# Seven products of halves in the projection of the layer embedding

## The chip, the core and the metric

The kernel runs on one core of a Trainium2 chip. The metric is the device time of one execution in microseconds (us), taken as the median of several runs of the same program. A separate execution was recorded by the hardware profiler, and every duration of a single instruction in this document comes from such a recorded execution. Engines are named as in the profile: PE (TensorE matmul), PEld (its weight load), DVE (VectorE), ACT (ScalarE), POOL (GpSimd), SP (the engine that issues all DMAs here).

## The reference, cut to what matters

The kernel computes one decoder layer on 1024 tokens of width 1024: a norm, an input projection, a mixture of dilated attention and a spatial gating unit, an output projection, a feed-forward network, and at the end a gated addition of a per-token layer embedding. The change touches the last factor of the last line:

```
h = h + rmsnorm(mixed, ln_post_mix[i])
...
h = h + rmsnorm(y, ln_post_ffn[i])
gate = jax.nn.sigmoid(h @ w_pe_gate[i] + b_pe_gate[i])
h = h + gate * (p[i] @ w_pe_proj[i])
```

`p[i]` is 1024 x 256 and `w_pe_proj[i]` is 256 x 1024, in 32-bit floats. This product depends on nothing else in the layer, so it can be computed at any time before the end.

## The kernel before, in words

Tokens are cut into eight row tiles of 128. A product of two float32 matrices is made of three matmuls on split operands: each operand is split into a rounded high part (an ACT copy into a rounding type) and the remainder as low part (a DVE subtraction), and `mm3` (L521) issues high x high, high x low and low x high into the same PSUM bank. A matmul takes a stationary operand of 128x128 and a moving one of up to 128x512.

Most products of the kernel also use a scheme with seven products of halves in place of eight: both matrices are cut into 2x2 blocks, some sums and differences of blocks are formed, seven block products are computed in the order `ORDER = (1, 2, 6, 5, 7, 3, 4)` (L660), and their results are added up in two PSUM banks and in SBUF. `winograd_b` (L650) forms the sums of the second operand in place, with four block additions. `gated(pair)` (L1063) does this for the spatial-gating half of the output projection, for two row tiles at a time.

The projection of the layer embedding did not use the scheme. `ple(t)` (L1125) handles one row tile t. It loads the 128x256 rows of p, transposes the two 128x128 blocks on PE, splits the result, and for each of the two column halves of 512 issues two `mm3` calls (one for each block of the contraction) into a bank of the group "fill". ACT copies the bank to SBUF, and SP stores it into the DRAM tensor `ppd`, which `embed` (L1462) reads at the end of the kernel. The first call also loads and splits w_pe_proj: four 512-wide splits.

The order of instructions is not written out by hand. The functions record operations in a graph, and a planner (`Graph.order`, L225) replays it on the host with priced operations and fixes one order for each engine. Its `pick` (L283) takes, on a free engine, the first operation in recorded order that is ready and whose tiles fit; for PE it looks at up to 80 waiting operations, for DVE and ACT at 40, and nothing further than 400 operations past the oldest unfinished one may take new tiles (L122 to L124). SBUF tiles come from pools: 47 tiles of kind M (4 KB in each partition) and 14 of kind S (2 KB); PSUM has 8 banks, kind P. Some groups have a limit of tiles at once, "fill" three banks (L1513).

What stands around the change is the attention. It is done for four pairs of heads: first the first 512 tokens (`first_half`, L1289, for pr 0 to 3), then the other 512 (`second_half`, L1304, with the steps "far", 2 and 3). After each unit of attention some independent work is recorded behind it, as filler: `fed` (L1285) advances generators, `feed` (L1267) counts down the numbers that they yield. The generator `others` (L1326) holds `gated` and `ple`. A first half feeds `FA` times 0.15 twice and `FA` times 0.35 twice; a second half feeds `FO` times 0.15, 0.12 and 0.23, twice each. `gated` yields 6 for each of its seven products (six matmuls each), `ple` yielded 7 for each column half (six matmuls and a transpose). A second filler, `ahead` (L1339, the first products of the gate and up projections), becomes available only after the far step of the second pair of heads, when the first four row tiles have gone through `attn_out` (L1148), `h_chain` (L1159) and `F.first2` (L591). What is left of `ahead` runs afterwards.

Of the kernel before, what the change touches and what calls it, by code (L numbers as in the profile page):

```python
# [12 lines left out]
F32R = mybir.dt.float32r  # L13
# [4 lines left out]
P = 128  # L18
S = 1024
D = 1024  # L20
NT = S // P
# [7 lines left out]
PLE = 256  # L29
# [3 lines left out]
LO, HI = slice(0, 512), slice(512, 1024)  # L33
ADD, SUB, MUL = ALU.add, ALU.subtract, ALU.mult
# [357 lines left out]
def hybrid_block(ctx: ExitStack, tc, a, out):  # L392
    G = Graph()

    def M(dt=F32, shape=(P, 1024), group=None):
        return G.buf("M", shape, dt, group)

    def SM(dt=F32, shape=(P, 512), group=None):
        return G.buf("S", shape, dt, group)

    def PB(shape=(P, 512), group=None):
        return G.buf("P", shape, F32, group)
# [4 lines left out]
    def C(shape):  # L407
        return G.buf("C", shape)
# [4 lines left out]
    def pe(what, *args, **kw):  # L413
        return G.call("tensor", what, *args, **kw)
# [4 lines left out]
    def load(dst, src, rate=1.0):  # L419
        o = G.call("sync", "dma_start", dst, src)  # L420
        o.bytes /= rate
        return o

    def tt(dst, x, y, op=ADD, engines="vector"):
        return G.call(engines, "tensor_tensor", out=dst, in0=x, in1=y, op=op)

    def copy(dst, src):
        return G.call("scalar", "copy", dst, src)
# [4 lines left out]
    def split(hi, lo, x, engines="vector"):  # L433
        copy(hi, x)
        tt(lo, x, hi.f32(), SUB, engines)
# [6 lines left out]
    w_pg, w_pp = a["w_pe_gate"][0], a["w_pe_proj"][0]  # L442

    def rows(w, k0, nk, c0, ncol):
        return w[k0 * P : (k0 + nk) * P, c0 : c0 + ncol].rearrange("(k p) n -> p k n", p=P)
# [9 lines left out]
    def piece_r(w, k0):  # L455

        return (1024, [rows(w, k0 + i, 1, 0, 1024) for i in range(2)])
# [31 lines left out]
    def weights(piece, gains=None):  # L489
        return split_raw(load_raw(piece), piece[0], "vector", gains)  # L490


    ident, mhalf = C([P, P]), C([P, 8])
# [27 lines left out]
    def mm3(ps, l, r, first, last, **kw):  # L521
        pe("matmul", ps, l[0], r[0], start=first, stop=False, **kw)
        pe("matmul", ps, l[0], r[1], start=False, stop=False, **kw)
        pe("matmul", ps, l[1], r[0], start=False, stop=last, **kw)

    def gemm(ps, terms):
        for i, (l, r) in enumerate(terms):
            mm3(ps, l, r, i == 0, i == len(terms) - 1)
        return ps
# [120 lines left out]
    def winograd_b(q, b, tmp):  # L650

        if q == 6:
            tt(b(0, 1), b(1, 1), b(0, 1), SUB)
            tt(b(0, 0), b(0, 1), b(0, 0))
        if q == 5:
            tt(tmp, b(1, 1), b(0, 0), SUB)
            tt(b(1, 0), b(1, 0), b(0, 0), SUB)
        return tmp if q == 5 else b(*{1: (0, 0), 2: (1, 0), 3: (1, 1), 4: (1, 0), 6: (0, 0), 7: (0, 1)}[q])

    ORDER = (1, 2, 6, 5, 7, 3, 4)  # L660


    x = a["x"][0]
# [63 lines left out]
    ppd, h1d = DR([S, D]), DR([S, D])  # L727
# [100 lines left out]
    for q, banks in in_products(2048, 1536, zu_mm):  # L828
        for i in range(4):
            if q in (1, 6, 5):  # L830
                v, t = {1: (zs, i), 6: (us, i), 5: (us, i + 4)}[q]
# [5 lines left out]
            else:  # L837
                v = {2: zs, 3: us}.get(q, us)[i + 4 * (q == 7)]
# [6 lines left out]
            if q in (3, 4):  # L845
                t = i + 4 * (q == 4)
# [273 lines left out]
                tt(dst, bank, dst)  # L1120
            yield 6

    p, wpp = a["p"][0][0], []

    def ple(t):  # L1125
        if t == 0:
            wpp.extend(weights(piece_r(w_pp, 0)))
        pt = SM()[:, :PLE]
        load(pt, p[t * P : (t + 1) * P, :])
        ps = PB((P, 2, P), "fill")  # L1130
        for k in range(2):
            pe("transpose", ps[:, k, :], pt[:, k * P : (k + 1) * P], ident)
        pair = SM(F32R, (P, 2, PLE))
        split(pair[:, 0], pair[:, 1], ps.flat())
        for cs in (LO, HI):
            ps = gemm(PB(group="fill"), [
                (tuple(pair[:, i, k * P : (k + 1) * P] for i in range(2)), tuple(v[:, cs] for v in wpp[k]))
                for k in range(2)
            ])
            pp = SM()  # L1140
            copy(pp, ps)
            load(ppd[t * P : (t + 1) * P, cs], pp)
            yield 7


    F, kept = Feat(), {}
# [37 lines left out]
                skip_group_check=True)  # L1184

    EARLY = 20
    FB, FH, FF2, FA, FO = 36, 0, 48, 30, 105
    TODO = (((0, "far"), ("h", 0)), ((0, "far"), ("h", 1)), ((0, 2), ("h", 2)), ((0, 2), ("h", 3)), ((1, "far"), ("f", 0)),
            ((1, "far"), ("f", 1)))
    ed = {n: DR([2 * P, 512]) for n in range(EARLY)}  # L1190
# [72 lines left out]
    def chain(*gens):  # L1263
        for g in gens:
            yield from g
# [38 lines left out]
    def second_half(pr, fills, then):  # L1304
# [10 lines left out]
        for step in ("far", 2, 3):  # L1315
# [6 lines left out]
            if step in then:  # L1322
                then[step]()
        merge(pr)

    others = chain(*(gated(i) for i in range(2)), *(ple(t) for t in range(2)), *(gated(i) for i in range(2, 4)),  # L1326
                   *(ple(t) for t in range(2, NT)))

    def rows_out(*ts):
        for t in ts:  # L1330
# [63 lines left out]
    one = [PB() for _ in range(4)]  # L1394
    for q in ORDER:
        if q in (2, 5):
            two = [PB() for _ in range(4)]
        banks = two if q in (2, 5, 3) else one
        for g in range(NG):
            for j, c in USED.get(q, ()):  # L1400
                cs = slice(c * 512, (c + 1) * 512)
# [4 lines left out]
            s = winograd_b(q, lambda j, c: w_raw[g, j][:, c * 512 : (c + 1) * 512], tmp)  # L1406
            if g % 2 == 0:
                n = min(2, NG - g)
# [61 lines left out]
    wq, one, two, c11, c12, c22 = {}, [PB() for _ in range(4)], [], {}, {}, {}  # L1470
# [8 lines left out]
    for i in range(4):  # L1479
        ps = PB()  # L1480
# [25 lines left out]
    for i in range(4):  # L1506
        gate_product(4, i, one[i], False, True)
        for c in (0, 256) if i == 3 else (0,):
            cs = slice(c, c + 256) if i == 3 else LO
# [50 lines left out]
```

## Time and profile before

| what | value |
|---|---|
| median of 3 runs | 1162.27 us (1162.27 to 1162.47) |
| the profiled execution, its own time | 1162.04 us |
| span from first to last instruction in it | 1160.2 us |
| granted TensorE clock, mean | 0.999 |
| DMA | 231.86 MB, mean 200 GB/s |

The span leaves out 1.84 us of the profiled execution's time, before the first and after the last instruction. In the profile, a row of a group gives the engine, the operation, what it writes and reads by kind of tile (m, s, t for the SBUF pools, p for PSUM, c for constants, d for DRAM), the shape, the count, the busy time of the group, the mean duration of one in ns, and the idle time of the engine ahead of them. The duration of a matmul is longer than the distance between two of them, because they are pipelined. A row of windows gives the busy time and the number of instructions of PE, PEld, DVE, ACT and POOL in a stretch of the span. All operations carry L386, the line of the helper that issues them, so groups are told apart by tiles and shapes.

### The profile page before, as it was taken

The numbers are of one execution on the slowest core, as the hardware profiler recorded it, in microseconds if no ns is written. First come the engines' busy times: TensorE is split into PE (matmuls) and PEld (weight loads), VectorE is DVE, ScalarE is ACT, GpSimd is POOL, SyncE is SP. The second block draws the span as 40 slices with busy tenths as digits, with TensorE's granted clock in tenths as the row PEclk, the third lists the DMA queues.
The fourth block names the chain that finished last, engine by engine and source line by source line (L and its number), as shares of the span: only waits on it lengthen the run. The fifth ranks groups of instructions, "written<-read, shape, count | busy, mean of one in ns | idle before, by whom it ended". The sixth has DMA issues, their size and how long they took to land.

```text
span 1160.2 us, 16519 instructions
## 1 busy us (share of the span) xinstructions
PE 1147.9 (99%) x5549; PEld 959.0 (83%) x5549; DVE 929.6 (80%) x1798; ACT 611.9 (53%) x1358; POOL 56.2 (5%) x67
## 2 busy tenths in 40 slices
PE   8999999999999999999999999999999999999998
PEld 6888888788888888888888888888888888888886
DVE  7978897787868767789888888877766897766898
ACT  7654438589959776555233223222345445654822
POOL 2001010000111000310000000000000000001100
PEclk9999999999999999999999999999999999999999
DMA  8133125999967986377456666646399844744355
GB/s 316 39 100 114 68 97 167 333 301 309 270 195 217 262 255 190 121 232 219 124 181 201 195 190 195 190 147 215 111 350 361 314 154 154 285 169 156 120 197 181
DMA packets 168430, 231.86 MB, mean 200 GB/s; under 512 B 13389, under 2 KB 90777, under 8 KB 168346
## 3 DMA queue, kind: packets, MB, share of 16 engines
q1 hardware_dynamic: 168346, 230.81, 61.6%
q8 instruction: 44, 0.72, 0.3%
q14 instruction: 40, 0.33, 0.1%
HBM read 160.21 MB, written 70.55 MB: 199 GB/s over the span
## 4 chain that ended last, share of the span: by engine, by line
PE 96%; ACT 2%; DVE 1%; DMA 1%; issue 0%; SPq 0%; DVEq 0%; ACTq 0%
PE p L386 96%; ACT m L386 2%; DMA m<-in_w_in 1%; DVE m L386 0%; ACT s L386 0%; DVE s L386 0%; SPq L386 0%; ACT t L386 0%; DVEq L386 0%; ACTq L386 0%
## 5 line engine op out<-in xcount | busy, mean ns | idle before, releaser
L386 PE MATMUL p<-m,m 128*128 128x512 f32 (+1 forms) x4536 | 1050.3, 389 | 1.6 <-DVE m L386 0.8
L386 PEld LDWEIGHTS p<-m,m 128*128 128x128 f32 x4536 | 835.7, 188 | 167.9 <-ACT m L386 2.9
L386 DVE TENSOR_TENSOR m<-m,m 128x512 fp32r<-128x512 f32 (+3 forms) x536 | 351.6, 691 | 56.9 <-ACT m L386 50.9
L386 ACT CAST m<-m 128x512 fp32r<-128x512 f32 (+1 forms) x409 | 232.0, 604 | 199.2 <-PE p L386 103.6
L386 DVE TENSOR_TENSOR s<-p,s 128x512 f32<-128x512 f32 (+4 forms) x238 | 152.7, 652 | 77.2 <-PE p L386 63.6
L386 ACT ACTIVATE s<-s 128x512 f32<-128x512 f32 (+1 forms) x71 | 44.2, 627 | 158.6 <-DVE s L386 118.6
L386 ACT COPY s<-p 128x512 f32<-128x512 f32 (+1 forms) x134 | 68.9, 521 | 42.9 <-PE p L386 38.1
L386 POOL TENSOR_TENSOR t<-t,c 128x1 f32<-128x1 f32 (+1 forms) x56 | 41.3, 743 | 1015.3 <-ACT t L386 946.0
L386 DVE TENSOR_TENSOR m<-p,m 128x512 f32<-128x512 f32 (+3 forms) x124 | 62.6, 523 | 34.0 <-ACT m L386 23.7
L386 DVE TENSOR_TENSOR m<-s,m 128x512 fp32r<-128x512 f32 (+2 forms) x121 | 74.0, 633 | 7.8 <-ACT m L386 7.3
L386 DVE TENSOR_TENSOR s<-s,s 128x512 f32<-128x512 f32 (+1 forms) x117 | 75.9, 657 | 5.2 <-ACT s L386 1.6
L386 ACT CAST m<-s 128x512 fp32r<-128x512 f32 (+1 forms) x117 | 65.9, 581 | 23.9 <-PE p L386 14.6
L386 ACT COPY m<-p 128x512 f32<-128x512 f32 (+2 forms) x106 | 48.9, 494 | 32.9 <-PE p L386 32.0
L386 PE MATMUL p<-c,m 128*128 128x128 f32 x328 | 50.3, 273 | 0.6 <-ACT t L386 0.6
L386 ACT ACTIVATE m<-m 128x1024 f32<-128x1024 f32 (+1 forms) x32 | 33.5, 1061 | 28.2 <-DVE m L386 20.9
L386 PE MATMUL p<-s,m 128*128 128x128 f32 (+1 forms) x256 | 44.8, 278 | 0.0
L386 PE MATMUL p<-c,s 128*128 128x128 f32 (+2 forms) x249 | 42.5, 278 | 2.1 <-DVE s L386 1.2
L386 PEld LDWEIGHTS p<-c,m 128*128 128x128 f32 x328 | 39.0, 140 | 6.3 <-ACT t L386 0.9
L386 PEld LDWEIGHTS p<-s,m 128*128 128x128 f32 x256 | 38.3, 190 | 3.1
L386 PEld LDWEIGHTS p<-c,s 128*128 128x128 f32 (+2 forms) x249 | 31.1, 143 | 10.7 <-DVE s L386 3.5
L386 ACT ACTIVATE m<-m,t 128x384 f32<-128x384 f32 (+2 forms) x64 | 37.0, 584 | 5.1 <-DVE t L386 4.9
L386 ACT CAST s<-p 128x512 fp32r<-128x512 f32 (+2 forms) x64 | 31.6, 524 | 11.7 <-PE p L386 11.4
(59 smaller groups left out, 490.4 us busy)
## 6 DMA issues: line engine op xcount, KB each, us to landing
d<-s SPq DMA_DIRECT2D x149, 256.0 KB, 3.3
m<-d SPq DMA_DIRECT2D x63, 512.0 KB, 4.9
d<-m SPq DMA_DIRECT2D x48, 512.0 KB, 5.2
m<-in_w_gate_up SPq DMA_DIRECT2D x88, 256.0 KB, 4.0
m<-d SPq DMA_DIRECT2D x87, 256.0 KB, 6.5
s<-d SPq DMA_DIRECT2D x71, 256.0 KB, 3.8
m<-in_w_down SPq DMA_DIRECT2D x44, 256.0 KB, 6.4
m<-in_w_in SPq DMA_DIRECT2D x20, 512.0 KB, 4.2
```

The costliest lines, as they stand in the source:

```text
L386: getattr(getattr(nc, o.engine), o.what)(*[real(v) for v in o.args], **{k: real(v) for k, v in o.kw.items()})
```

## The change

`ple` now takes four row tiles in one call (`four` is 0 or 1). The four tiles of p are cut into an upper and a lower pair and into their two 128-wide blocks; w_pe_proj is cut into 2x2 blocks of 128x512. Seven products of halves, each one `mm3`, are issued for each i in 0, 1, and their results are added up in PSUM and in tiles of kind S. All `gated` calls are recorded ahead of the two `ple` calls, and the feeding constants FA and FO change. The diff, whole:

```diff
@@ -1120,27 +1120,68 @@
-    p, wpp = a["p"][0][0], []
-
-    def ple(t):
-        if t == 0:
-            wpp.extend(weights(piece_r(w_pp, 0)))
-        pt = SM()[:, :PLE]
-        load(pt, p[t * P : (t + 1) * P, :])
-        ps = PB((P, 2, P), "fill")
-        for k in range(2):
-            pe("transpose", ps[:, k, :], pt[:, k * P : (k + 1) * P], ident)
-        pair = SM(F32R, (P, 2, PLE))
-        split(pair[:, 0], pair[:, 1], ps.flat())
-        for cs in (LO, HI):
-            ps = gemm(PB(group="fill"), [
-                (tuple(pair[:, i, k * P : (k + 1) * P] for i in range(2)), tuple(v[:, cs] for v in wpp[k]))
-                for k in range(2)
-            ])
-            pp = SM()
-            copy(pp, ps)
-            load(ppd[t * P : (t + 1) * P, cs], pp)
-            yield 7
+    p, wpp = a["p"][0][0], {}
+
+    def ple(four):
+
+
+        if four == 0:
+            raw = [M(group="raw") for _ in range(2)]
+            for j in range(2):
+                load(raw[j], w_pp[j * P : (j + 1) * P])
+            for q in ORDER:
+                w = winograd_b(q, lambda j, c: raw[j][:, c * 512 : (c + 1) * 512], SM() if q == 5 else None)
+                hl = M(F32R, (P, 2, 512))
+                split(hl[:, 0], hl[:, 1], w)
+                wpp[q] = hl[:, 0], hl[:, 1]
+        turned = []
+        for i in range(2):
+            t, ps = 4 * four + 2 * i, PB((P, 4, P))
+            pt = SM()
+            load(pt.split(PLE), p[t * P : (t + 2) * P, :].rearrange("(t p) c -> p t c", p=P))
+            for k in range(2):
+                for j in range(2):
+                    pe("transpose", ps[:, 2 * k + j, :], pt[:, j * PLE + k * P : j * PLE + (k + 1) * P], ident)
+            turned.append(ps.flat())
+        x, s, d = SM(), SM(), SM()
+        x1, x2, s1, s2, d3, d7 = (v[:, c : c + 256] for v in (x, s, d) for c in (0, 256))
+        parts = {}
+
+        def halves(qs, v):
+            hl = M(F32R, (P, 2, 512))[:, :, : v.n]
+            split(hl[:, 0], hl[:, 1], v)
+            for n, q in enumerate(qs):
+                parts[q] = [tuple(hl[:, h, c : c + P] for h in range(2)) for c in range(256 * n, 256 * n + 256, P)]
+
+        copy(x, turned[0])
+        halves((1, 2), turned[0])
+        copy(d7, turned[1][:, :256])
+        tt(s1, turned[1][:, 256:], d7)
+        tt(s2, s1, x1, SUB)
+        halves((4,), turned[1][:, 256:])
+        halves((5, 6), s)
+        tt(d7, x1, d7, SUB)
+        tt(d3, x2, s2, SUB)
+        halves((3, 7), d)
+        for i in range(2):
+            got, one = {}, PB(group="fill")
+            for n, q in enumerate(ORDER):
+                if q in (2, 5):
+                    two = PB(group="fill")
+                bank = two if q in (2, 5, 3) else one
+                mm3(bank, parts[q][i], wpp[q], q in (1, 2, 5), True, skip_group_check=True)
+                at = {1: (0, LO), 2: (0, LO), 6: (0, HI), 3: (0, HI), 5: (1, HI), 7: (1, HI), 4: (1, LO)}[q]
+                if q in (1, 6, 5, 4):
+                    got[q] = SM()
+                    copy(got[q], bank)
+                else:
+                    tt(got[{2: 1, 3: 6, 7: 5}[q]], bank, got[{2: 1, 3: 6, 7: 5}[q]])
+                if q in (2, 3, 7, 4):
+                    t = 4 * four + 2 * at[0] + i
+                    load(ppd[t * P : (t + 1) * P, at[1]], got[{2: 1, 3: 6, 7: 5, 4: 4}[q]])
+                if n % 2:
+                    yield 6
+            yield 3
@@ -1184,7 +1225,7 @@
-    FB, FH, FF2, FA, FO = 36, 0, 48, 30, 105
+    FB, FH, FF2, FA, FO = 36, 0, 48, 26, 70
@@ -1323,8 +1364,7 @@
-    others = chain(*(gated(i) for i in range(2)), *(ple(t) for t in range(2)), *(gated(i) for i in range(2, 4)),
-                   *(ple(t) for t in range(2, NT)))
+    others = chain(*(gated(i) for i in range(4)), ple(0), ple(1))
```

## The prediction, made before the changed kernel was run

> **What bounds the kernel now.** I read the page's busy times first, then the timeline of PE in a quiet stretch, then the windows around the place where the changed code runs, and last the waits of PE there. The page:
>
> ```profile
> span 1160.2 us, 16519 instructions
> PE   1147.9 (99%) x5549; PEld 959.0 (83%) x5549; DVE 929.6 (80%) x1798; ACT 611.9 (53%) x1358; POOL 56.2 (5%) x67
> ```
>
> PE is busy almost always, but a busy PE can hide waits, so I look at its pace. In the timeline (start, duration, engine, operation, count) one row covers 100 us of the gate and up projections:
>
> ```profile
> 599.74 100.58 PE L386 MATMUL p<-m,m 128*128 128x512 f32 x443
> ```
>
> With about 0.39 us for the last one's own duration, 442 distances take 100.19 us: 0.2267 us for each 512-wide matmul, without a gap. That is the price of a matmul where PE sets the pace. A matmul taken away there is 0.227 us off the end. The Trainium skill (TensorE: Matmul & The Clock Gate, "Wait — 56ns, not 53.3ns?") gives N ÷ 2.4 GHz plus about 2.5 ns, 215.7 ns at 512. This trace does not agree, it has 226.7 ns; by the page the PE term below would be 2.59 us.
>
> The old `ple` can be picked out of the groups kept apart by shape, because only its matmuls read a 512-wide m tile against a stationary s tile, and only its splits make a 256-wide rounded s tile out of p with these counts. The rows are its matmuls, its low parts and its high parts,
>
> ```profile
> L386 PE MATMUL p<-m,s 128*128 128x512 f32 x96 | 26.9, 408 | 0.5 <-ACT s L386 0.3
> ...
> L386 DVE TENSOR_TENSOR s<-p,s 128x256 fp32r<-128x256 f32 x8 | 3.3, 419 | 0.5 <-ACT s L386 0.5
> ...
> L386 ACT CAST s<-p 128x256 fp32r<-128x256 f32 x8 | 2.9, 377 | 0.0
> ```
>
> and the timeline row of its longest run:
>
> ```profile
> 355.58 5.28 PE L386 MATMUL p<-m,s 128*128 128x512 f32 x22
> ```
>
> The run has a distance of (5.28 - 0.40) / 21 = 0.232 us, nearly the quiet stretch's. It also says that for 5 us PE had nothing else to do than this filler: the attention was waiting for other engines.
>
> The windows around that place (length, then busy and count of PE, PEld, DVE, ACT, POOL, then clock and DMA):
>
> ```profile
> 228.00:326.00 98.00, 97.66 (x590) 84.72 (x590) 78.61 (x231) 83.44 (x240) 5.19 (x9) 1.00 0.98 290
> ```
>
> ```profile
> 318.00:345.00 27.00, 27.00 (x139) 22.62 (x139) 16.44 (x29) 15.46 (x43) 5.05 (x6) 1.00 0.73 219
> 345.00:370.00 25.00, 24.24 (x146) 20.87 (x145) 22.21 (x60) 20.54 (x60) 4.44 (x5) 1.00 0.60 181
> 370.00:381.00 11.00, 10.88 (x75) 9.54 (x74) 6.47 (x16) 10.12 (x24) 0.00 (x0) 1.00 0.90 218
> ```
>
> From 345 to 370 DVE is at 89% and ACT at 82%, and PE has 0.76 us of idle time. Its waits there, and the one ahead of the first old `ple` matmul, in the timeline (in brackets the idle time and what ended it):
>
> ```profile
> 263.56 0.50 PE L386 MATMUL p<-m,s 128*128 128x512 f32 x1 [0.34 <-ACT s L386]
> ...
> 353.82 0.30 PE L386 MATMUL p<-c,m 128*128 128x128 f32 x1 [0.65 <-ACT t L386]
> ```
>
> So the kernel is bound by PE, and the changed code lies in the stretch where PE depends most on having filler.
>
> **The change part by part.** *Matmuls.* Before: 8 row tiles x 2 column halves x 2 blocks x 3 = 96, as the row counts. After: 2 calls x 2 values of i x 7 products x 3 = 84. Twelve go: 12 x 0.2267 = 2.72 us (at the run's 0.232: 2.78). Transposes stay at 16.
>
> *Order of the filler.* In the first halves, 0.15 x 26 = 3.9 and 0.35 x 26 = 9.1 draw one and two yields of 6, as 4.5 and 10.5 did with yields of 6 and 7. So FA changes nothing, and 26 yields of six matmuls are drawn before and after: before 14 of `gated`, 4 of `ple`, 8 of `gated`; after 26 of `gated`. In the far half of the first pair of heads the old code drew 6 + 12 yields, 108 matmuls. The new one leaves 2 of `gated` and all of `ple`: steps of 10.5, 8.4 and 16.1 draw 24, 21 and 42 matmuls, 87, and the last 9 come in the far step of the second pair. All twelve removed matmuls are thus taken from the filler of one stretch, about 318 to 381 us.
>
> *DVE and ACT.* The rows for the new operations (the 512-wide low part and rounding, the combination with a bank, the copies out of PSUM, a 256-wide rounding, a 256-wide sum):
>
> ```profile
> L386 DVE TENSOR_TENSOR m<-m,m 128x512 fp32r<-128x512 f32 x374 | 249.4, 694 | 51.6 <-ACT m L386 49.9
> L386 ACT CAST m<-m 128x512 fp32r<-128x512 f32 x377 | 221.0, 621 | 182.0 <-PE p L386 103.6 <-DVE m L386 66.0 <-issue 4.2
> L386 DVE TENSOR_TENSOR s<-p,s 128x512 f32<-128x512 f32 x162 | 111.2, 688 | 65.8 <-PE p L386 63.6 <-ACT m L386 0.9 <-ACT s L386 0.9
> ...
> L386 ACT COPY s<-p 128x512 f32<-128x512 f32 x90 | 53.0, 591 | 34.9 <-PE p L386 30.3 <-DMA d<-s 3.0 <-ACT s L386 0.5
> ...
> L386 ACT COPY s<-p 128x256 f32<-128x256 f32 x44 | 16.5, 378 | 8.0 <-PE p L386 7.8
> ...
> L386 ACT CAST m<-p 128x256 fp32r<-128x256 f32 x28 | 9.7, 474 | 0.0
> ...
> L386 DVE TENSOR_TENSOR s<-s,s 128x256 f32<-128x256 f32 x14 | 5.8, 417 | 0.2 <-ACT s L386 0.2
> ```
>
> DVE, at 0.69 and 0.42 us: the weights take 4 sums and 7 low parts, 11 x 0.69 = 7.6, for 4 x 0.69 = 2.8 before: +4.8. Each call takes 3 x 0.69 + 5 x 0.42 = 4.2 for its rows and 6 x 0.69 = 4.1 for combinations, 16.6 for both; before, 8 x 0.42 = 3.4. Net: +18 us. ACT: weights 7 x 0.62 for 4 x 0.62; each call 0.59 + 3 x 0.62 + 0.38 + 0.47 + 8 x 0.59 = 8.0, 16.0 for both, for 8 x 0.38 + 16 x 0.59 = 12.5. Net: +5.4 us.
>
> None of this is on the path if it finds room. Weight preparation depends on two loads alone, so it can be done ahead, in 228 to 326, where DVE has 19.4 us free of 98. In 318 to 381 DVE had 45.1 us of work in 63. Added there: 16.6, less six old low parts (2.5), less the two combinations of the `gated` yields that moved to the first halves (1.4): +12.7, 57.8 us in a stretch that should last 60.3. ACT: 46.1 + 16.0 - 9.4 - 1.2 = 51.5. It fits, at 96% and 85%, and this is where my doubt lies. That DVE can be full without PE waiting is shown by the first of these windows (the second is used for the range):
>
> ```profile
> 40.00:60.00 20.00, 20.00 (x96) 16.67 (x95) 19.82 (x34) 12.69 (x23) 0.00 (x0) 1.00 0.04 14
> ...
> 220.00:240.00 20.00, 18.68 (x106) 15.44 (x105) 16.53 (x44) 17.80 (x44) 0.00 (x0) 1.00 1.05 397
> ```
>
> There PE has plenty of ready work, though; near 355 it hasn't. So the cost lies between nothing and what overflows (below); and a gain is possible too, if the new order removes waits of 263.56 and 353.82 and the 0.12 of 370 to 381: at most 0.34 + 0.76 + 0.12 = 1.2 us. I take nothing, as the windows leave room and give no reason for a gain.
>
> *Transfers.* Rows of the DMA view (KB each, median us to landing):
>
> ```profile
> m<-in_c_bias SPq DMA_DIRECT2D x8, 448.0 KB, 5.2
> ...
> m<-in_w_pe_proj SPq DMA_DIRECT2D x2, 512.0 KB, 8.0
> s<-in_p SPq DMA_DIRECT2D x8, 128.0 KB, 6.6
> ```
>
> The eight loads of p become four of 256 KB, the two of w_pe_proj move from 246 us to later, and the sixteen stores of 256 KB remain. Share of the DMA engines is 0.98 in 228 to 326, where they are full, and 0.60 to 0.90 after it: no cost, and no gain that PE would see, as it is idle 0.34 us in those 98.
>
> *Waits inside the new code.* Seven products go through two banks, three matmuls (0.68 us) each. The next product into the same bank is queued on PE behind the copy or combination that empties it (0.59 or 0.69), and PE's tail of 0.39 - 0.23 = 0.16 and some 0.1 for two hand-overs come on top: about 0.9, so 0.2 us stays open where nothing else is ready. `gated` does the same with six matmuls (1.36 us), which covers it. Softmax steps stand behind the same copies on ACT and DVE. Covered by attention work and by product 5, which has a fresh bank: I take 0, at most 0.2 x 15 = 3 us, for the 46 matmuls that ran with little else from 355 to 369.
>
> **Sum.** 1162.04 of the profiled execution - 2.72 = 1159.32; the median of before is 0.23 above its profiled execution, so 1159.55: forecast 1159.6 us.
>
> **The rivals.** *The filler runs short.* The time from 345 to 370 may be set by DVE and ACT, with PE merely filled up; then twelve matmuls fewer become 2.7 us of idle time, or the bank waits (up to 3 us) take them back: 1162.3, no change. For it: DVE at 89%, the run of 22. Against it: PE idles only 0.76 us, and 9 matmuls now reach beyond the stretch.
>
> *DVE overflows.* From 345 to 381 DVE had 28.7 us of work in 36, 7.3 free. If all 12.7 fall there, 5.4 too many delay the norms that open the second filler: 1162.3 + 5.4 = 1167.7. It costs something from 7.3 on, and is measurably slower (0.2%, about what a measurement of this kernel can tell from no change, is 2.3 us) from 9.6 on. Against it: half of the new rows (call 0) can use the 10.6 us free in 318 to 345.
>
> *Tiles run out.* Counted in recorded order, up to 39 of the 47 M tiles live in this half with 4 of old weights; the new code has 7 for weights and 4 for rows, up to 46. Then a load for the next pair of heads is issued late, and one exposed bias load is 5.2 us: 1159.6 + 5.2 = 1164.8. Against it: the first halves hold 4 tiles fewer.
>
> *Headroom on PE.* PEld is at 83%, so PE may not be the limit at all, and the change moves nothing: 1162.3. Against it: the gapless stretch has the same share, 0.188 of 0.2267 us. The Trainium skill (Perfetto Trace Analysis, "Identifying the Most-Contended Engine") says to judge TensorE by weight-load busy and not by matmul busy, which is where this reading comes from; the trace does not bear it out here.
>
> **How the numbers follow.** Forecast, faster: 0.46. Filler short, between 1160.0 and 1164.6: 0.32, headroom 0.02: together no change 0.34. DVE overflow 0.12 and tiles 0.08: slower 0.20. Range: below, the sum with those waits gone and also the 1.3 us that PE idles from 220 to 240, where the first gated rows are late and the planner is as free to order anew: 1159.6 - 1.2 - 1.3 = 1157.1. Above, into the dear cases up to the tiles' price, 1165.0; about 0.16 is left out. The forecast's own range is 1157.1 to 1159.9.
>
> **What would show it.** Right: the 0.2267 us pace unchanged, the p<-m,s group of 96 gone and 84 more of p<-m,m, PE idle in 228 to 400 not above 2 us, DVE's total near 948 us, ACT's near 617. Wrong by short filler: PE idle time of 2 us or more between 345 and 385, ended by ACT or DVE. Wrong by overflow: DVE without gaps from 340 to 385 and the second filler starting after 381. Wrong by tiles: an idle PE ended by a DMA.

## The result, and the profile after

The changed kernel takes 1165.30 us (median of 11 runs, 1164.82 to 1166.68); the kernel before took 1162.35 beside it. The ratio is 1.0026 [1.0019, 1.0034]: slower by 3.0 us, against a forecast of 1159.6 and a range that ended at 1165.0. The profiled execution took 1165.30, 3.26 more than that of before; its mean granted clock is the same 0.999.

The page after, span and busy times:

```profile
span 1163.5 us, 16523 instructions
PE 1148.1 (99%) x5537; PEld 956.6 (82%) x5537; DVE 944.2 (81%) x1825; ACT 615.5 (53%) x1365; POOL 57.0 (5%) x67
```

PE has twelve instructions fewer (5537 for 5549) and is no less busy. DVE has 14.6 us more and ACT 3.6 more. The matmul group, kept apart by shape, first of the kernel before, then of the kernel after:

```profile
L386 PE MATMUL p<-m,m 128*128 128x512 f32 x4352 | 1023.3, 392 | 1.6 <-DVE m L386 0.8 <-ACT m L386 0.6
```

```profile
L386 PE MATMUL p<-m,m 128*128 128x512 f32 x4436 | 1050.0, 393 | 4.6 <-DVE m L386 2.5 <-ACT m L386 1.5 <-ACT s L386 0.3
```

84 more of them, as the new projection issues, and the group of 96 (p<-m,s) is gone. The pace where PE sets it has not changed; a timeline row of the gate and up projections after:

```profile
594.63 115.53 PE L386 MATMUL p<-m,m 128*128 128x512 f32 x509
```

508 distances in 115.14 us are 0.2267 us each, as before. What grew in the group is the last column: PE waited 1.6 us ahead of these matmuls, and now 4.6 us. To find where, the windows of before and then of after (length, then busy and count of PE, PEld, DVE, ACT, POOL, then clock, DMA share, GB/s):

```profile
228.00:300.00 72.00, 71.66 (x452) 62.90 (x452) 59.08 (x189) 64.34 (x188) 2.72 (x5) 1.00 1.01 312
300.00:326.00 26.00, 26.00 (x141) 21.82 (x140) 19.52 (x43) 19.10 (x54) 2.48 (x4) 1.00 0.89 228
345.00:381.00 36.00, 35.13 (x219) 30.41 (x218) 28.68 (x76) 30.65 (x83) 4.44 (x5) 1.00 0.70 192
228.00:400.00 172.00, 170.78 (x1025) 147.53 (x1025) 133.88 (x378) 141.24 (x400) 14.13 (x18) 1.00 0.89 262
```

```profile
228.00:300.00 72.00, 72.00 (x447) 63.16 (x447) 61.76 (x193) 65.03 (x186) 2.19 (x4) 1.00 1.04 318
300.00:326.00 26.00, 23.70 (x134) 18.47 (x133) 23.82 (x56) 23.20 (x67) 3.28 (x4) 1.00 0.41 127
345.00:381.00 36.00, 34.35 (x207) 28.23 (x206) 33.48 (x84) 31.49 (x86) 5.52 (x6) 1.00 0.99 296
228.00:400.00 172.00, 168.05 (x998) 142.28 (x998) 147.01 (x392) 145.25 (x406) 15.01 (x18) 1.00 0.87 259
```

PE's idle time in 228 to 400 went from 1.22 to 3.95 us. Most of it is new in 300 to 326, where before there was none and after there is 2.30; DVE there went from 75% to 92% and ACT from 73% to 89%. The rest is in 345 to 381 (0.87 to 1.65). PE's waits after, in 228 to 400 (total, times, longest):

```profile
PE p L386 <- DVE m L386: 1.7, 3, 0.9
PE p L386 <- ACT m L386: 0.9, 2, 0.5
PE p L386 <- DVE s L386: 0.6, 3, 0.2
PE p L386 <- ACT s L386: 0.5, 2, 0.3
PE p L386 <- DVE t L386: 0.3, 1, 0.3
```

All are ended by DVE or ACT, none by a DMA. Transfers moved all the same: in the windows the DMA share falls from 0.89 to 0.41 in 300 to 326 and rises from 0.70 to 0.99 in 345 to 381. SP issues the first of the two bias loads for the second pair of heads 17 us later, before and after:

```profile
328.47 0.52 SPq L386 DMA_DIRECT2D m<-in_c_bias  x1
```

```profile
345.41 0.54 SPq L386 DMA_DIRECT2D m<-in_c_bias  x1
```

What DVE does in 300 to 326 is in its timeline (start, duration), of before and then of after. The operation m<-m,c,m belongs to the weights of the output projection, m<-p,t,m is a result of that projection, and s<-m,m of 512 is a sum in the new weight preparation:

```profile
307.36 1.51 DVE L386 SCALAR_TENSOR_TENSOR m<-m,c,m 128x512 fp32r<-128x512 f32 x2 [1.34 <-ACT s L386]
...
315.87 0.74 DVE L386 SCALAR_TENSOR_TENSOR m<-m,c,m 128x512 fp32r<-128x512 f32 x1
...
319.01 0.75 DVE L386 SCALAR_TENSOR_TENSOR m<-p,t,m 128x512 f32<-128x512 f32 x1 [1.12 <-PE p L386]
```

```profile
301.42 0.68 DVE L386 TENSOR_TENSOR s<-m,m 128x512 f32<-128x512 f32 x1
...
307.21 0.69 DVE L386 TENSOR_TENSOR m<-m,m 128x512 fp32r<-128x512 f32 x1
...
310.37 0.68 DVE L386 TENSOR_TENSOR m<-m,m 128x512 fp32r<-128x512 f32 x1
...
315.71 1.42 DVE L386 SCALAR_TENSOR_TENSOR m<-m,c,m 128x512 fp32r<-128x512 f32 x2
...
323.75 0.74 DVE L386 SCALAR_TENSOR_TENSOR m<-m,c,m 128x512 fp32r<-128x512 f32 x1
...
325.75 0.75 DVE L386 SCALAR_TENSOR_TENSOR m<-p,t,m 128x512 f32<-128x512 f32 x1 [0.31 <-PE p L386]
```

The new weights are prepared from 295 to 311 us, among the last units of attention of the first halves: three of the eleven DVE operations stand before 300, eight behind. The output projection's weights come 8 us later than before, and its first result 6.7 us later. PE's timeline after shows the attention waiting in the same place:

```profile
308.30 0.50 PE L386 MATMUL p<-m,m 128*128 128x256 f32 x2 [0.28 <-DVE t L386]
308.98 1.11 PE L386 MATMUL p<-s,m 128*128 128x128 f32 x8 [0.18 <-DVE s L386]
...
313.06 0.96 PE L386 MATMUL p<-m,m 128*128 128x512 f32 x3 [0.92 <-DVE m L386]
...
316.20 1.66 PE L386 MATMUL p<-m,m 128*128 128x512 f32 x6 [0.30 <-ACT s L386]
```

Idle time is only part of the loss, since a matmul that starts a little late behind another leaves no gap in these rows. Counted for each matmul from 220 to 470 us is the distance to the next start less the median distance of its shape and kinds of tile: 7.7 us before and 14.0 after (0.6 and 4.6 of it in 300 to 330, 2.0 and 4.4 in 350 to 380). That is 6.3 us more lost, of which 2.7 show as idle time; with 2.72 us of matmuls gone it gives +3.6, and +3.26 was measured. I call this sum the *time lost on PE* below.

### The profile page after: what moved, and what is told of

Its sections match the earlier page's. It is cut to its first block, busy times and chain, and to the rows that moved or that the text cites. A ratio compares the mean times of both kernels' runs of the same rounds, so it can differ in the third digit from the quotient of the medians.

```text
span 1163.5 us, 16523 instructions
## 1 busy us (share of the span) xinstructions
PE 1148.1 (99%) x5537; PEld 956.6 (82%) x5537; DVE 944.2 (81%) x1825; ACT 615.5 (53%) x1365; POOL 57.0 (5%) x67
## 4 chain that ended last, share of the span: by engine, by line
PE 93%; ACT 3%; DVE 2%; DMA 1%; issue 0%; SPq 0%; POOL 0%; DVEq 0%; ACTq 0%
PE p L386 93%; ACT m L386 2%; DVE m L386 1%; ACT s L386 1%; DMA m<-in_w_in 1%; DVE s L386 0%; SPq L386 0%; POOL t L386 0%; ACT t L386 0%; DVE t L386 0%; DVEq L386 0%; ACTq L386 0%
## 5 line engine op out<-in xcount | busy, mean ns | idle before, releaser
L386 PE MATMUL p<-m,m 128*128 128x512 f32 (+2 forms) x4620 | 1075.4, 390 | 5.1 <-DVE m L386 2.5
L386 PEld LDWEIGHTS p<-m,m 128*128 128x128 f32 x4620 | 849.5, 189 | 176.4 <-ACT m L386 4.3
L386 DVE TENSOR_TENSOR m<-m,m 128x512 fp32r<-128x512 f32 (+2 forms) x540 | 354.0, 691 | 54.1 <-ACT m L386 48.6
L386 DVE TENSOR_TENSOR s<-p,s 128x512 f32<-128x512 f32 (+3 forms) x244 | 158.6, 659 | 76.1 <-PE p L386 63.3
L386 DVE TENSOR_TENSOR m<-p,m 128x512 fp32r<-128x512 f32 (+3 forms) x128 | 64.8, 524 | 32.1 <-ACT m L386 21.1
L386 DVE TENSOR_TENSOR m<-s,m 128x512 fp32r<-128x512 f32 (+2 forms) x126 | 77.6, 635 | 9.6 <-ACT m L386 8.9
L386 ACT CAST m<-s 128x512 fp32r<-128x512 f32 (+1 forms) x122 | 68.9, 581 | 26.8 <-PE p L386 17.6
L386 DVE TENSOR_TENSOR s<-s,s 128x512 f32<-128x512 f32 (+1 forms) x123 | 78.3, 645 | 5.2 <-ACT s L386 1.5
L386 PEld LDWEIGHTS p<-c,s 128*128 128x128 f32 (+2 forms) x249 | 30.8, 143 | 10.9 <-DVE s L386 3.7
L386 DVE SCALAR_TENSOR_TENSOR m<-m,t,m 128x1024 f32<-128x1024 f32 x24 | 30.5, 1279 | 4.7 <-POOL t L386 4.7
```

The lines of the kernel that those rows point to most:

```text
L386: getattr(getattr(nc, o.engine), o.what)(*[real(v) for v in o.args], **{k: real(v) for k, v in o.kw.items()})
```

## The experiments

My theory once the result was known: a removed matmul is worth its time, but the preparation, moved late by the new order, and the added DVE and ACT work hold up the attention. The rivals: the filler runs short (a removed matmul is worth nothing here), or the order itself is worse. "Old" is the projection of before, "new" that of the change; a kernel of before was run beside each.

| run | median us | before | ratio, 95% | lost on PE, 220 to 470 |
|---|---|---|---|---|
| the change | 1165.30 | 1162.35 | 1.0026 [1.0019, 1.0034] | 14.0 |
| old_gated_first | 1165.54 | 1162.22 | 1.0031 [1.0020, 1.0042] | 10.9 |
| old_gated_first_early | 1162.73 | 1162.43 | 1.0000 [0.9991, 1.0008] | 7.9 |
| old_84 | 1159.79 | 1162.22 | 0.9978 [0.9969, 0.9987] | 7.8 |
| old_gated_first_early_84 | 1159.92 | 1162.37 | 0.9978 [0.9969, 0.9987] | 7.8 |
| new_weights_early | 1163.49 | 1162.22 | 1.0008 [0.9999, 1.0016] | 10.5 |
| new_weights_mid | 1168.63 | 1162.24 | 1.0056 [1.0043, 1.0068] | |
| new_weights_after_feed | 1164.46 | 1162.40 | 1.0015 [1.0007, 1.0024] | 13.0 |
| old_84_load | 1166.38 | 1162.37 | 1.0032 [1.0020, 1.0045] | 15.0 |
| old_84_load_small | 1166.12 | 1162.24 | 1.0032 [1.0019, 1.0045] | |
| old_84_load_unpriced | 1169.56 | 1162.24 | 1.0062 [1.0048, 1.0075] | |
| new_small_sums | 1164.81 | 1162.43 | 1.0019 [1.0010, 1.0028] | 13.2 |
| new_early_bare | 1161.53 | 1162.37 | 0.9995 [0.9986, 1.0004] | 12.8 |
| new_bare_after_feed | 1162.48 | 1162.40 | 0.9998 [0.9989, 1.0007] | 11.5 |
| new_old_feed | 1172.51 | 1162.22 | 1.0086 [1.0072, 1.0100] | |
| new_early_80 | 1164.11 | 1162.43 | 1.0013 [1.0005, 1.0022] | |
| new_early_pool | 1163.44 | 1162.43 | 1.0008 [0.9999, 1.0016] | |
| new_early_finefeed | 1162.91 | 1162.37 | 1.0007 [0.9998, 1.0016] | |
| new_finefeed_after_feed | 1166.35 | 1162.40 | 1.0032 [1.0019, 1.0045] | |

**The order alone.** old_gated_first takes the old projection and only records all gated rows ahead of it:

```diff
-    others = chain(*(gated(i) for i in range(2)), *(ple(t) for t in range(2)), *(gated(i) for i in range(2, 4)),
-                   *(ple(t) for t in range(2, NT)))
+    others = chain(*(gated(i) for i in range(4)), *(ple(t) for t in range(NT)))
```

> The old projection (eight products, one row tile a call), but all gated calls recorded ahead of it; feeding constants as before. If the new order is what costs (the first halves now filled by gated rows alone), about 1165. If the cost lies in the new projection's own work on DVE and ACT, or in its fewer matmuls, within 0.5 us of the kernel before, 1162.3.

It costs 3.3 us, as much as the change lost, with 96 matmuls still there. PE's timeline of this run, at the first matmuls of the projection:

```profile
330.94 0.66 PE L386 MATMUL p<-c,m 128*128 128x128 f32 x4 [0.67 <-DVE m L386]
332.46 0.73 PE L386 MATMUL p<-m,s 128*128 128x512 f32 x2 [0.87 <-DVE s L386]
```

The second row is the old projection waiting for the split of its rows. The four weight splits stand at 294 to 299 us in this run (260 to 265 before). The time lost on PE is 0.6 us above that of before in 300 to 330, 1.1 above in 330 to 350 and 1.4 in 350 to 380, so it lies behind the splits and not beside them. Next, old_gated_first_early records the four weight splits right after `prepare_low(0)`, ahead of the attention:

```diff
-        if t == 0:
-            wpp.extend(weights(piece_r(w_pp, 0)))
...
     prepare_low(0)
+    wpp.extend(weights(piece_r(w_pp, 0)))
     feed(others, 12)
```

> The old projection with all gated calls first, and the four splits of its weights recorded ahead of the attention. If the new order costs 3.3 us only because it moves the weight preparation beside the first attention outputs, this is back at the kernel before, 1162.3 to 1163. If the order costs because of the filler itself (gated rows in the first halves, projection rows in the second), 1165.

The loss is gone: 1162.73 with the same order of rows. So it isn't gated rows ahead of the projection that cost, but the place of the weight preparation, which had moved with the projection. How a place at 294 to 299 costs time behind 330 isn't shown; the planner orders everything anew around it.

**Fewer matmuls alone.** old_84 is the kernel before with 84 matmuls in place of 96:

```diff
+            ps = PB(group="fill")
+            for k in range(2):
...
+                if k == 0 or t < 2:
+                    mm3(ps, l, r, k == 0, k == 1)
+                else:
+                    pe("matmul", ps, l[0], r[0], start=False, stop=False)
+                    pe("matmul", ps, l[0], r[1], start=False, stop=True)
```

> The kernel before with 84 of its 96 projection matmuls: for the row tiles from 2 on the low x high matmul of the second block is left out, and nothing else changes. If a matmul of this filler is worth its 0.227 us, 1162.3 - 2.7 = 1159.6. If the stretch is set by ACT and DVE and the filler only covers it, 1162.3.

The gain is 2.43 us, 0.20 for each matmul. Its page has PE 2.9 us less busy than before:

```profile
span 1157.9 us, 16498 instructions
PE   1145.0 (99%) x5537; PEld 956.1 (83%) x5537; DVE 928.6 (80%) x1798; ACT 611.2 (53%) x1358; POOL 55.9 (5%) x67
```

So here a removed matmul of the filler is worth most of its time, which refutes the short filler. old_gated_first_early_84 joins the last two edits, the order, the early weights and the 84 matmuls:

> The old projection with gated rows first, weights prepared ahead of the attention, and 84 of its 96 matmuls (the same twelve left out). If order, weight position and matmul count are all that the change does to the path, this shows what the seven products would give without their extra sums and copies: 1159.6 to 1160. If the fewer matmuls hurt in this order, 1162 or more.

1159.92: nearly the forecast's gain, in the change's order. What new_weights_early below has beyond it is the added DVE and ACT work with its tiles, the new grouping and the smaller FA and FO.

**The place of the weights in the changed kernel.** The preparation becomes a function, and is called in three places: right after `prepare_low(0)` (new_weights_early), after the first draw of gated rows behind it (new_weights_after_feed), and after the first half of the second pair of heads (new_weights_mid):

```diff
     prepare_low(0)
+    ple_weights()      # new_weights_early
     feed(others, 12)
+    ple_weights()      # new_weights_after_feed
     for pr in range(4):
...
         first_half(pr, [(others, FA)], {0: nxt})
+        if pr == 1:
+            ple_weights()      # new_weights_mid
```

> The changed kernel with the preparation of the seven weight blocks (two loads, four sums, seven splits) recorded ahead of the attention in place of the end of its first halves. If the bunch of preparation on ACT and DVE at 300 to 325 us starves PE, most of the 4 us of waits there go: about 1162. If the filler is too short or the two banks are the cost, 1165 as the changed kernel.

> The changed kernel with its weight preparation recorded after the first half of the second pair of heads, in the middle of 228 to 326 us, where I had counted 19 us of free DVE time. If only the place beside the first attention outputs costs, 1163.5 as with early weights. If preparation costs anywhere among the attention, 1165 to 1168.

> The new projection with its weight preparation recorded right after the first two draws of gated rows, where new_weights_early has it right ahead of them. In new_weights_early and its variants PE waits 1.76 us for DVE at 225 to 228 us, 1.32 in the kernel before, and in two of their profiles (new_early_80, new_early_finefeed) the granted clock falls to 0.50 for 3.4 us right behind it, which loses 1.71 us; most executions of new_weights_early have a mean clock of 0.998 and lie 1.5 us above those of 1.000. Theory: the gated rows come late because the weights stand ahead of them on DVE, and the longer wait makes the clock fall in many executions. Then with the gated rows first the wait is 1.4 us or less, the clock stays at 0.999 or more, and the median is 1162.1, the executions within 1 us. Rival: the spread between the executions has another cause, and the median stays at 1163.5 with a spread of 2 us. Third: from here the weights slide into the attention, and cost part of the 3 us that the recorded order of the change costs: 1164 or more, with PE waits at 300 to 330.

Early, it returns 1.8 us by the medians, and 3.3 in the two profiled executions (1162.01 for 1165.30; the first is the fastest of its eleven). The window that had lost most:

```profile
300.00:326.00 26.00, 25.95 (x154) 22.18 (x153) 19.77 (x50) 20.92 (x59) 2.65 (x3) 1.00 0.88 277
```

PE's idle time there is back to 0.05 us, and the time lost on PE in 300 to 330 from 4.6 to 0.8. Recorded among the attention, the same work costs more than in the change itself (1168.63); a draw later than early, 1164.46. It is the same 7.6 us of DVE and 4.3 of ACT each time.

I had expected new_weights_after_feed at 1162.1, for another reason. Executions of new_weights_early fall apart: three took 1162.0 to 1162.2 at a mean clock of 0.999 or more, and the seven at 0.998 took 1163.4 to 1164.2. The eleventh doesn't fit: 1163.4 at 0.999. In a variant with the same early weights and a wait of PE at the same place (new_early_finefeed), the windows show what a lower mean is made of:

```profile
224.00:226.00 2.00, 1.19 (x9) 0.85 (x8) 2.00 (x5) 2.00 (x6) 0.00 (x0) 1.00 1.06 400
226.00:228.00 2.00, 1.15 (x8) 0.73 (x8) 2.00 (x5) 2.00 (x7) 0.00 (x0) 0.96 1.10 389
228.00:230.00 2.00, 1.89 (x5) 1.53 (x6) 2.00 (x5) 1.73 (x5) 0.00 (x0) 0.50 1.07 395
230.00:232.00 2.00, 2.00 (x8) 1.57 (x7) 1.43 (x4) 0.89 (x2) 0.00 (x0) 0.69 1.04 423
232.00:234.00 2.00, 2.00 (x10) 1.64 (x9) 1.33 (x4) 0.37 (x1) 0.00 (x0) 1.00 1.04 424
```

PE idles 1.66 us in 224 to 228, and then the granted clock is half for about 3.4 us: 1.71 us lost, about what lies between the two groups of executions. With the preparation behind the first draw PE waits 0.99 us there, and all 11 executions are at 0.999 or more, as expected of the clock; they still spread over 2.2 us, not 1. The median rose: the last three weight splits then stand at 231 to 234 us, beside the first units of attention, and the time lost on PE in 300 to 330 is 2.4, though the preparation ends 66 us ahead of it. In new_weights_mid it ends at 268, and 1.8 are lost there. So the loss in 300 to 330 isn't only DVE and ACT being taken up in that stretch; the order that the planner makes behind the preparation may have a part in it, and no run separates the two. The clock loss is probably a part of what separates the early version's median from its best executions; it doesn't explain what separates those best executions, at 1162.0, from the forecast.

**What added DVE work costs.** old_84_load gives old_84 unused DVE additions on the copied results, nothing waiting for them; old_84_load_small has the same recorded order and cuts them to 16 columns; old_84_load_unpriced has them full, at a price of 0.02 us for the planner:

```diff
             copy(pp, ps)
+            if t >= 2:
+                junk = SM()
+                tt(junk, pp, pp)
+                tt(junk[:, :256], pp[:, :256], pp[:, 256:])
```

> The kernel before with 84 matmuls (low x high of the second block left out for the row tiles from 2 on), plus one 512-wide and one 256-wide DVE addition into an unused tile for each of those twelve column halves: 12 x (0.69 + 0.42) = 13.3 us of DVE work in the same stretch, on which nothing waits. If DVE work in this stretch is free as long as nothing waits for it, 1159.8 as with 84 matmuls alone. If the stretch has no room for it, most of what the seven products cost comes back: 1163 to 1166.

> The kernel old_84_load in exactly its own order of instructions, but its 24 unused DVE additions work on 16 columns, about 2 us in place of 13.3. If the additions cost by the time they take on DVE, back to 1160 to 1161. If they cost by what they displaced in the planner's order (priced at their full width), it stays at 1165 to 1166.

> The kernel old_84_load with the same 24 additions at full width, but priced at 0.02 us for the planner, so that it orders the rest nearly as without them. If DVE time itself is what the stretch lacks, 1164 to 1166. If the displaced order was the cost, 1160 to 1162.

The 24 additions, 11.2 us by DVE's totals (939.8 less 928.6), cost 6.6. The windows of this run:

```profile
326.00:345.00 19.00, 19.00 (x103) 15.84 (x102) 17.30 (x36) 14.18 (x38) 4.66 (x5) 1.00 0.61 209
345.00:381.00 36.00, 32.34 (x186) 27.84 (x186) 31.15 (x83) 27.80 (x74) 4.01 (x4) 0.91 0.66 187
```

Where DVE is at 91% beside a steady filler (326 to 345) PE loses nothing; in 345 to 381 it is at 87%, and PE idles 3.66 us. In the chain of steps there PE waits four times in a row, twice for DVE, once for ACT and once, by the profile, for a store out of a tile of kind S:

```profile
367.78 0.41 PE L386 MATMUL p<-c,s 128*128 128x128 f32 x2 [1.34 <-DVE t L386]
368.52 0.33 PE L386 MATMUL p<-c,s 128*128 128x128 f32 x1 [0.33 <-ACT s L386]
369.39 0.33 PE L386 MATMUL p<-c,s 128*128 128x128 f32 x1 [0.53 <-DMA d<-s]
371.12 1.77 PE L386 MATMUL p<-s,m 128*128 128x128 f32 x8 [1.40 <-DVE s L386]
```

Behind these waits the clock is half for 7 us, which loses 3.4 us more (below). Idle time in 206 to 416 rose by 3.15 us over old_84, and with 3.42 of clock that is the 6.6. Cutting the additions short in that order gives 0.3 back. So in that order it isn't DVE's time in the additions that costs, but what both kernels share: the order that the planner made for the additions, or the tile of kind S that each pair of them takes. Leaving them out of the planner's prices makes it 3.2 dearer, above both of the times that I had expected; this is a third order with the full additions, and it doesn't tell DVE's time from the order.

new_small_sums does the same cut on the changed kernel: its own order, with the twelve combinations with a bank cut to 16 columns:

```diff
-                    tt(got[{2: 1, 3: 6, 7: 5}[q]], bank, got[{2: 1, 3: 6, 7: 5}[q]])
+                    tt(got[{2: 1, 3: 6, 7: 5}[q]], bank, got[{2: 1, 3: 6, 7: 5}[q]]).cut = True
```

> The changed kernel in exactly its own order of instructions, but each of the twelve combinations of a bank with a tile (DVE, 512 wide) works on 16 columns only, which leaves out the rest of these sums: about 12 x 0.56 = 6.7 us less DVE work, no wait, bank or instruction removed. If DVE's load between 300 and 381 us is what makes PE wait, 1162 to 1163. If the cost lies in where the preparation stands in the order, within 1 us of the changed kernel, 1165.

Six us of DVE time less return 0.5: in the change's own order too, little of the loss is DVE's time in the combinations. new_early_bare goes further: early weights, no combinations at all, and the second call uses the row parts of the first, planned anew; new_bare_after_feed is that with the weights behind the first draw:

```diff
+        parts = shared[0] if four else ple_rows(0)
+        shared.append(parts)
...
-                else:
-                    tt(got[{2: 1, 3: 6, 7: 5}[q]], bank, got[{2: 1, 3: 6, 7: 5}[q]])
```

> The changed kernel with early weights, without the twelve combinations of banks with tiles and with the second call using the rows of the first, which leaves out its loads, transposes, sums and splits: some 12 us less DVE work, 3 us less ACT work and 0.9 us less on PE. If the remaining cost is the DVE and ACT work of rows and combinations, 1160 to 1161.5. If it is the bank alternation or the feed, 1162.5 or more.

> new_early_bare (no combinations with a bank, second call with the row parts of the first: leaves out 8.2 us of DVE work in combinations and the second call's rows) with the weight preparation behind the first two draws. If helper work of rows and combinations is what holds the new projection above the forecast, this comes to 1160.0 to 1160.7, the lower executions of new_early_bare, once the clock and the two load waits of that kernel (2.7 us on p in its profile) are gone. If something that it still has (two banks in turn, the grouping by products, the draws) holds it, it stays at 1161.5 or above without clock loss.

Against its partner with the full work each is 2.0 us faster (1163.49 to 1161.53, 1164.46 to 1162.48). But the bare kernels also leave out eight transposes on PE (5529 matmuls and transposes for 5537), which the old projection has as well: at 0.109 us from one to the next some 0.9 us. So an estimate of the price of the helper work on DVE and ACT, that half of the rows and the combinations, is 1.1. Neither came down to 1159.9.

**The draws.** Four arrangements of the same work: new_old_feed keeps the change with the old FA and FO (30 and 105); the other three have early weights: new_early_80 with FO 80, new_early_pool with sums and low parts of the rows on POOL where it is free, new_early_finefeed with a yield of 3 after each product and 21, 6 and 21 drawn after the three steps. new_finefeed_after_feed is the last one with the weights behind the first draw.

> The changed kernel with the feeding constants of before (FO 105 for 70, FA 30 for 26). If the thinner feeding leaves PE without filler, about 1162 to 1163. If the cost is the preparation of weights and rows, or the emptying of banks, it stays at 1165 or gets worse, since more of that work falls together.

> The changed kernel with weights prepared ahead of the attention, and FO 80 for 70, which draws the filler a little earlier. If the remaining waits come from too thin a feed, about 1162.5; if from DVE's load near 355 us, 1163.5 as with FO 70, or worse.

> The changed kernel with weights prepared ahead of the attention, FO 70, and the sums and low parts of p that lie in SBUF allowed on POOL as well as on DVE. If DVE's load near 355 us makes the remaining waits, about 1162 or a little below the kernel before; if not, 1163.5.

> The changed kernel with early weights, a yield after each product, and 21, 6 and 21 fed in the steps far, 2 and 3 of the second halves. The best arrangement of the new projection that I have: 1161.5 to 1162.5, so level with the kernel before or a little ahead. If DVE's load costs in any arrangement, not below 1161.5.

> new_early_finefeed with the same move of the weight preparation behind the first two draws. The clock theory: 1162.3, which is what the executions of new_early_finefeed with a clock of 0.999 gave, with all executions near it. If the waits for the rows' helper work after 345 us are what is left, it can't go much below: about 2.2 us of it remain against the 1159.9 of the kernel with early weights and 84 plain matmuls. Rival (another cause of the spread): 1162.9, spread 2 us and more.

With the old draws the 84 matmuls are used up too soon, and PE is without filler in the last step:

```profile
382.77 0.48 PE L386 MATMUL p<-c,m 128*128 128x128 f32 x1 [2.55 <-ACT m L386]
383.75 0.90 PE L386 MATMUL p<-c,m 128*128 128x128 f32 x3 [0.50 <-ACT m L386]
385.41 1.22 PE L386 MATMUL p<-m,m 128*128 128x512 f32 x2 [0.76 <-ACT m L386]
```

That is +7.2 over the change, up to 3.4 of it in 6.8 us of half clock from 382 us on, and more than I had expected of thin feeding or of the preparation. So the smaller FA and FO are a needed part of the change. The other early ones lie at 1162.9 to 1164.1; the best, new_early_finefeed, is level with before. Moving its weights by one draw made it 3.4 dearer, again with PE waits in 300 to 345 (1.06 us for DVE at 338).

## Why the prediction was wrong, by its own steps

- *Matmuls, 12 x 0.2267 = 2.72 us.* Right in mechanism, near in size: 2.43 in old_84 and 2.45 in old_gated_first_early_84.
- *Order of the filler.* That all gated rows first cost nothing as an order is borne out: with early weights it is level (1.0000). But the prediction moved the gated rows and left out that the projection's weights move with its first call, past the last units of the first halves.
- *DVE +18, ACT +5.4.* 14.6 and 3.6 by the totals; the forms were right, the amounts somewhat too high. The sums add whole durations, but neighbours on DVE overlap: after, two additions of 0.69 us start 0.60 apart, at 300.82 and 301.42.
- *"None of this is on the path if it finds room."* This step failed, twice: it put the added work at nothing because DVE and ACT had free time. It said that the preparation could be done in 228 to 326, where DVE had 19.4 us free of 98. It was done there, at 295 to 311, and PE lost 4.0 us more in 300 to 330 (0.6 to 4.6). The old projection, with its preparation moved late in the same way, lost 3.3, and the early recording took it back to level. The new one's took back 1.8 by the medians, 3.3 by the profiles. Then it said that 57.8 us of DVE work fit into 60.3 from 318 to 381. They fit, and the changed kernel with early weights is still 3.6 above 1159.92; by the estimate above, 1.1 of it is the helper work that the bare kernels leave out. Why free time isn't room is argued and not shown. My reading is that it's a sum of short gaps between steps that wait for one another, so that each operation put between them moves steps behind it, and that PE has no filler to spare for each delay. Shortening the additions in a fixed order gave back only 0.3 and 0.5, so the price lies more in the order than in DVE's time. The trace it leaned on, DVE full at 40 to 60 with PE never idle, was a stretch with other ready work, as the prediction itself noted.
- *Waits inside the new code 0, transfers 0.* No wait of PE in 228 to 400 is ended by a DMA after. The banks were not tried by themselves.
- *A gain of up to 1.2 from waits removed.* The wait at 263.56 did go: 228 to 300 has PE busy for 72.00 of 72. New ones behind it, 2.30 in 300 to 326 and 0.78 more in 345 to 381, outweigh it.
- *Rivals.* Short filler (1162.3): refuted by old_84. Headroom on PE: refuted by the same run. Tiles (1164.8): their sign, an idle PE ended by a DMA, is absent in 228 to 400, but they aren't refuted. Each kernel here with the new projection issues that first bias load at 334 to 346 us, and each one with the old at 328 to 333; after the change ACT also waits 1.16 us, at 338.8, for a store out of a tile of kind M. No run tells whether tiles hold up the attention or a late attention the loads. DVE overflow (1167.7): the nearest, since PE's new waits are ended by DVE and ACT, but its point of 7.3 us from which it decides was wrong. In 345 to 381 DVE took 4.8 us more, 33.48 of 36, and the time lost on PE in 350 to 380 still rose by 2.4.

The account: 1159.9 is reached with plain matmuls, 5.4 us below the change. The late preparation is 1.8 of them by the medians, and half of the rows with all combinations about 1.1. The other 2.5 stay open: new_early_bare is 1.6 above 1159.92 with 0.9 less on PE. The remaining rows, two banks in turn, the grouping of the draws, the tiles, a clock of 0.998 in three of its executions, and 2.7 us of waiting for p in its profiled one all can be in it. Each new arrangement is ordered anew by the planner, which by the draws above moves the time by about 1 us, and once by 3.4, so terms of that size can't be told apart here. The 1.8 and the 2.0 of the bare kernels aren't far above it; for them speaks that the second came out alike in two arrangements, and that early weights returned 2.8 in the old projection.

## What to carry to other kernels

In a stretch where PE runs on filler beside a chain of short dependent steps, a matmul saved was worth most of its time (0.20 of 0.227 us), but the helper work that it costs isn't free just because DVE and ACT have gaps: put a dummy load of the same size there first and see whether it costs. Here 11.2 us of it cost 6.6, and the change, with 14.6 us more on DVE, ended 5.4 above plain matmuls. Then cut the load short in its own order, to see whether its time or the order is what costs. Preparation that depends on loads alone belongs ahead of such a stretch; when a step is moved, look at which first call carries its preparation. And look at the granted clock behind each cluster of waits before putting a loss down to the waits alone.

## What the runs showed of the hardware

A cluster of short waits of PE can cost its length again in clock. The windows of 2 us of old_84_load, where PE idles 3.60 us in 366 to 372:

```profile
366.00:368.00 2.00, 0.66 (x7) 0.41 (x4) 2.00 (x10) 2.00 (x8) 0.00 (x0) 1.00 0.97 204
368.00:370.00 2.00, 0.85 (x4) 0.28 (x2) 1.33 (x7) 2.00 (x8) 0.00 (x0) 1.00 1.04 331
370.00:372.00 2.00, 0.89 (x5) 0.89 (x6) 1.63 (x6) 2.00 (x8) 0.00 (x0) 0.84 1.08 207
372.00:374.00 2.00, 1.94 (x10) 1.54 (x10) 2.00 (x7) 1.50 (x7) 0.00 (x0) 0.50 0.18 21
374.00:376.00 2.00, 2.00 (x11) 2.00 (x10) 1.15 (x4) 1.51 (x4) 0.00 (x0) 0.50 0.07 2
376.00:378.00 2.00, 2.00 (x11) 1.95 (x10) 1.94 (x4) 2.00 (x5) 0.00 (x0) 0.50 0.73 143
378.00:380.00 2.00, 2.00 (x12) 1.66 (x12) 2.00 (x5) 0.83 (x2) 0.00 (x0) 0.95 0.49 123
```

The clock is half from about 371 to 378 us, a loss of 3.42 us; in every profile that has it the loss is 1.71 or 3.42, one or two pieces of 3.4 us at half (the last few us of the span, where every profile has the half clock, left aside). The Trainium skill (TensorE: Matmul & The Clock Gate, "What's actually happening") gives a free-running window of 3.413 us and half rate as the only other state; these rows agree with the length and the rate. The rule that the Trainium skill names (TensorE: Matmul & The Clock Gate, "HAM oscillation — how this bites in real kernels") is no idle gaps of over about 3.4 us. Here shorter ones were enough: waits of 0.65, 0.16 and 0.96 us close together did it in new_early_finefeed at 225 to 228. Waits of that size stand there in the profiles of five kernels with early weights: two of them (the other is new_early_80) have the half clock, and new_weights_early, new_early_pool and new_early_bare kept the full one, so near the edge it differs by execution. The 1.32 us in the kernel before, at the same place, never brought it in a profile here.
